# Longer pauses in the matmul order of a hybrid attention and linear-attention step: four places

## The chip, the cores and the metric

The kernel runs on one core of one Trainium2 chip. A core has a matrix engine (PE in the profile, with its weight loads as PEld), a vector engine (DVE), a scalar engine (ACT), a general engine (POOL), and a sync engine (SP) that issues most of the transfers. The metric is the time of one execution on the device, in microseconds (us). The times of several executions of the same program are compared by their median.

## The reference

One step of a layer with two groups of heads side by side. All arrays are float32; there are 2048 prompt rows and 32 rows of a running stream ("sample").

```python
n = rmsnorm(x)
z = n @ w_in                       # 1024 -> qa, ka, va, qg, kg, vg, rg, ca
# group A: 8 query heads, 2 key heads of 64; each chunk of 64 rows sees two chunks back
s = q @ k.T / 8 ; m = max(max(s), sink)
p = exp(s - m) ; a = p / (sum(p) + exp(sink - m)) @ v
# group B: 4 heads, keys of 64, values of 128; a decay for each key element
log_a = log_sigmoid(ca @ w_alpha + b_alpha) / 16
S = exp(log_a) * S + k v.T ; o = q S          # chunk-wise in the reference
g = rmsnorm(o) * silu(rg)
h = x + concat(a, g) @ w_out
y = h + relu(rmsnorm(h) @ w_up)**2 @ w_down   # 1024 -> 4096 -> 1024
```

The outputs are y for prompt and sample, the last keys and values, and the two states S.

## The kernel before

Rows are worked in tiles of 128: tile 0 to 15 are the prompt, tile 16 is the sample. A float32 product is made of three matmuls on pieces of the operands (high x high, high x low, low x high; names end in h and l). The program has four stages: attention (to about 372 us of the profiled execution), linear attention (to about 695 us), the output projection (to about 870 us), and the two layers of the feed-forward part.

**The order on PE is written at build time.** `self.clock` (L140 to L175) is a running sum of what the emitted matmuls should take, in ns. Large products (`gemm`, `gemm_wide`) call `tick()` after every few matmuls. Attention of a tile (`attend`, L607), a tile of linear attention (`gla_tile`, L990 and on) and the decay of a half (`decay`, L841) are generators: each `yield ns` is a pause, and `tick()` resumes a generator when `self.clock` has passed its due time. So a longer pause puts more matmuls of the large product that is running between two pieces of a generator. The order so made is fixed on PE by dependences between neighbours (`_pe`). The order on DVE, ACT, POOL and SP is made afterwards by a scheduler of the language, from the program as a whole; an engine runs its own list strictly in order. No instruction moves at run time.

**Attention.** For each tile the products zq, zkv and zr are made (query, key and value, gate), DVE normalizes queries and keys into qk and kn (L510, L512). `attend` then pauses (L608), transposes them (`qTp`, `kTp`), pauses, makes scores S for two chunks of 64 rows, each with the exponentials P on ACT behind the maxima and negm on DVE (L654, L655), and pauses after each chunk (L674). After a further pause come the transposes of P (pT), their copies to SBUF on ACT (pS), and the outputs O. S, pT, O and the small products of linear attention all live in one PSUM pool (`ps_s`) of five banks; a new tile in it waits until the readers of an older one are done. The large products use another pool (`ps_m`) of three.

**Linear attention.** It goes by halves of two tiles; half 0 has the sample tile as well. For a half, `project` makes zq, zk and zv. `decay` pauses (L855) and makes the gate logits la (two matmuls), which ACT and DVE turn into cc, a running sum (L871, L875). Each `gla_tile` then makes POOL, ACT and DVE build the arrays E from cc, q and k (L1023, L1034). On PE: small products dk for the diagonal, which DVE writes into AT (L1046); two transposes, also into the bank dk; 52 small matmuls A, which DVE masks into AT (L1099); a pause (L1104); and then go, the output, with v, AT, the query and the state. From go follow the new state (L1131), squares on ACT, a sum on DVE (L1138), an inverse root in many small steps (L256 to L261), and g (L1143), whose four operations are the last readers of go's two banks. After a long pause g is transposed (gTp). Several tiles are thus in flight, with DVE between most of their steps.

Of the kernel before, what the change touches and what calls it, by code (L numbers as in the profile page):

```python
# [66 lines left out]
class Builder:  # L67
# [240 lines left out]
    def attention_phase(self):  # L308
        tc, a, V, S, G, Q = self.tc, self.a, self.V, self.S, self.G, self.Q
        nt = self.nt  # L310
        w_in = a["w_in"].rearrange("(k p) n -> p k n", p=P)
        with ExitStack() as ctx:
# [103 lines left out]
            h, l = self.tok_pair("nT_0", 2 * P)  # L416
# [124 lines left out]
            def transposed_qk(t, qk, kn, ca):  # L541
                r = self.rows(t)
                pt = self.ps_s(f"qTp_{t}").rearrange("p (j t) -> p j t", j=4)[:, :, :r]
                for j in range(4):
                    self.tr(pt[:, j], qk[:r, j].rearrange("p v d -> p (v d)"))
                pk = self.ps_s(f"kTp_{t}")
                self.tr(pk[:, :r], kn[:r])
                self.tr(pk[:96, P : P + r], ca[:r].bitcast(F32))
                caT = wk.tile([96, P], F32, tag="caT", name=f"caT_{t}", bufs=1)
                V.tensor_copy(caT[:, :r], pk[:96, P : P + r])  # L550
                Q.dma_start(self.cad[t], caT[:, :r])
                return pt, pk[:, :r]
# [52 lines left out]
                self.store_mix(nt, slice(0, 4), aT)  # L605

            def attend(t, qk, kn, v, ca):  # L607
                yield 8500  # L608
                pt, pk = transposed_qk(t, qk, kn, ca)
                qT = wk.tile([P, 2, 4, 64], F32, tag="qT", name=f"qT_{t}")  # L610
                V.tensor_scalar(
# [18 lines left out]
                for ch in range(2):  # L630
# [36 lines left out]
                    for _, a0, m in parts[ch]:  # L667
# [3 lines left out]
                        if m == 64:  # L671
                            src, rb = (x.rearrange("p (v jp) k -> p v jp k", v=2) for x in (src, rb))
                        (G if ch == 0 else V).tensor_tensor(out=dst, in0=src, in1=rb, op=ALU.mult)  # L673
                    yield 3000  # L674
                yield 2000
                o = self.ps_s(f"O_{t}").rearrange("p (j t) -> p j t", j=4)
                for ch in range(2):
# [36 lines left out]
            for i, t in enumerate(order):  # L714
# [20 lines left out]
                if t == nt - 1:  # L735
# [5 lines left out]
                    Q.dma_start(self.rsd, rsT)  # L741
                    self.prepare_gla(0)
                self.spawn(attend_sample(*z.pop(t)) if t == nt else attend(t, *z.pop(t)))
                if t != nt - 2:
                    project_gate(t)
# [95 lines left out]
    def decay(self, h, tail=None):  # L841
# [10 lines left out]
        for t in tiles:  # L852
            Q.dma_start(ca[:, off : off + self.rows(t)].bitcast(F32), self.cad[t])
            off += self.rows(t)
        yield 5000 + 4000 * (h == 0)  # L855
        cc = self.cc[h] = self.mid.tile([P, 2, 288], F32, tag="cc", name=f"cc_{h}")
        if N <= 2 * P:
            x = self.ps_s(f"la_{h}")
# [20 lines left out]
    def gla_phase(self):  # L879
        tc, a, V, S, G, Q = self.tc, self.a, self.V, self.S, self.G, self.Q  # L880
        nt = self.nt
        with ExitStack() as ctx:
# [95 lines left out]
            def after(n, s):  # L978
                for _ in range(60):
                    if n < 0 or stage[n] >= s:  # L980
                        return
                    yield 500
                reach(n, s)
# [6 lines left out]
            def gla_tile(n, t, off, kq, cc):  # L990
# [9 lines left out]
                first = key == "p" and t == 0  # L1000
# [100 lines left out]
                                src[r].rearrange("s p (n m) -> s p n m", m=m),  # L1101
                            )
                stage[n] = 2
                yield 10000 if t != nt - 1 else 5000  # L1104
                yield from after(n - 1, 3)
                yield from after(n - 2, 4)

# [946 lines left out]
```

## Time and profile before

| what | value |
|---|---|
| median of 3 runs | 2169.01 us (2164.01 to 2177.4) |
| the profiled execution | 2172.5 us |
| its span, first to last instruction | 2170.7 us |
| mean granted PE clock | 0.992 |
| linear attention, 372 to 695 us: PE busy | 308.14 of 323.00 us |
| feed-forward, 870 to 2170.7 us: PE busy | 1286.57 of 1300.70 us |

The span is the time from the first to the last instruction of one execution that the profiler recorded; the execution took 1.8 us more than its span. A row of the page gives for a group of instructions the busy time, the mean of one, and the idle time of its engine just ahead of them with what ended it. In a timeline row the idle time stands in square brackets. The granted clock is a share of PE's full speed: at 0.50 every matmul takes twice its time.

### The profile page before, as it was taken

Reading aid. Unit: us, or ns where it says so; the run is one execution under the profiler, and the core shown is the slowest. Engines: PE = TensorE matmul, PEld = TensorE weight load, DVE = VectorE, ACT = ScalarE, POOL = GpSimd, SP = SyncE. Lnnn points to the kernel's source line nnn. Section 1 sums busy time; section 2 is a strip of 40 time slices with the busy share of each in tenths; the row PEclk is TensorE's granted clock in tenths of the full one; section 3 lists DMA queues with packets and bytes.
Section 4 is the critical chain, followed back from the end, with each engine's and each line's share of the span. In section 5 each row is a group of like instructions: output and inputs, shape, how many; then the busy total and the mean of one; then the engine's idle time right before and its main releaser. Section 6 shows DMA issues by size and latency. Waiting matters only on the chain.

```text
span 2170.7 us, 40621 instructions
## 1 busy us (share of the span) xinstructions
PE 2128.6 (98%) x14826; PEld 2002.9 (92%) x14826; DVE 1520.8 (70%) x3388; ACT 1231.6 (57%) x2737; POOL 1496.9 (69%) x1409
## 2 busy tenths in 40 slices
PE   8999999999998999999999999999999999999999
PEld 6777786788887999999999999999999999999999
DVE  7766766889997444677777775666666756776665
ACT  6554555565664222666665666656566666666663
POOL 1354445545553677889888786777887768888887
PEclk9999999999999999999999999999999999999999
DMA  8344565244435986765454467444444584445443
GB/s 287 128 159 133 188 209 170 104 166 143 158 104 162 378 325 273 284 194 164 154 158 161 136 211 249 130 140 130 140 146 127 179 286 136 139 149 155 145 127 108
DMA packets 189097, 381.81 MB, mean 176 GB/s; under 512 B 32209, under 2 KB 117378, under 8 KB 182114
## 3 DMA queue, kind: packets, MB, share of 16 engines
q1 hardware_dynamic: 154130, 323.10, 44.8%
q10 hardware_dynamic: 28208, 27.77, 3.7%
q0 software_dynamic: 6560, 28.35, 3.6%
q8 instruction: 117, 1.92, 0.4%
q14 instruction: 82, 0.67, 0.1%
HBM read 282.40 MB, written 96.76 MB: 175 GB/s over the span
## 4 chain that ended last, share of the span: by engine, by line
PE 87%; DVE 5%; DMA 4%; ACT 2%; issue 1%; POOL 1%; SPq 0%; ACTq 0%; DVEq 0%; POOLq 0%
PE dn L170 28%; PE u L170 27%; PE op L170 8%; PE zq L170 5%; PE zv L170 4%; PE zr L170 4%; PE zkv L170 2%; PE zk L170 2%; PE O L170 1%; PE go L170 1%; PE S L170 1%; PE A L170 1%; DVE AT L1099 1%; DMA stage<-in_w_in 1%; PE pT L174 1%
## 5 line engine op out<-in xcount | busy, mean ns | idle before, releaser
L1658 DVE TENSOR_TENSOR P<-P,dn 128x712 f32<-128x712 f32 (+1 forms) x612 | 534.5, 875 | 234.4 <-PE dn L170 218.1
L44 ACT ACTIVATE u<-u 128x356 f32<-128x356 f32 (+1 forms) x384 | 173.8, 453 | 43.5 <-PE u L170 23.2
L44 ACT ACTIVATE r<-u 128x356 f32<-128x356 f32 (+1 forms) x189 | 87.3, 462 | 132.0 <-PE u L170 131.9
L1658 DVE TENSOR_TENSOR u<-u,r 128x356 f32<-128x356 f32 (+1 forms) x144 | 75.7, 525 | 114.0 <-PE u L170 97.7
L1551 POOL TENSOR_TENSOR stage<-stage 128x512 f32<-128x512 f32 x90 | 117.0, 1300 | 22.5 <-DMA stage<-in_w_up 17.6
L1023 POOL TENSOR_TENSOR E<-cc 128x256 f32<-128x256 f32 (+1 forms) x117 | 70.0, 632 | 76.3 <-DVE cc L875 42.7
L792 POOL TENSOR_TENSOR sd<-sd 128x128 f32<-128x128 f32 (+2 forms) x132 | 94.5, 724 | 30.7 <-DMA sd<-in_w_down 26.6
L1099 DVE COPY_PREDICATED AT<-masks,A 64x64 f32<-64x64 int32 (+1 forms) x330 | 82.9, 253 | 16.1 <-ACT AT L44 5.8
L1658 DVE TENSOR_TENSOR uT<-u,uT 128x356 fp32r<-128x356 f32 (+1 forms) x183 | 89.9, 511 | 5.9 <-ACT uT L44 5.9
L44 ACT ACTIVATE uT<-u 128x356 fp32r<-128x356 f32 (+1 forms) x187 | 81.1, 457 | 3.0 <-DVE u L1658 2.8
L1658 DVE TENSOR_TENSOR uB<-u,uB 128x356 fp32r<-128x356 f32 (+1 forms) x141 | 72.3, 513 | 9.2 <-ACT u L44 8.5
L44 ACT ACTIVATE P<-S,negm 128x192 f32<-128x192 f32 (+2 forms) x128 | 51.6, 417 | 46.4 <-DVE negm L655 36.8
L44 ACT ACTIVATE op<-y 128x356 f32<-128x356 f32 (+1 forms) x42 | 19.4, 468 | 95.1 <-DVE y L1406 94.9
L1406 DVE TENSOR_TENSOR y<-op,y 128x356 f32<-128x356 f32 (+1 forms) x48 | 24.8, 529 | 67.0 <-PE op L170 62.7
L44 ACT ACTIVATE E<-E 128x1024 f32<-128x1024 f32 (+2 forms) x68 | 67.3, 1013 | 1.1
L44 ACT ACTIVATE uB<-u 128x356 fp32r<-128x356 f32 (+1 forms) x141 | 64.6, 458 | 2.9
L673 POOL TENSOR_TENSOR P<-P,es 128x512 f32<-128x512 f32 x15 | 15.5, 1036 | 68.3 <-ACT sq L44 27.2
L1034 DVE TENSOR_TENSOR E<-E,kq 128x256 f32<-128x256 f32 (+1 forms) x117 | 59.5, 561 | 0.7 <-ACT E L44 0.6
L44 ACT ACTIVATE pS<-pT 128x256 f32<-128x256 f32 (+1 forms) x62 | 27.2, 490 | 43.3 <-PE pT L174 43.3
L44 ACT ACTIVATE v<-go 128x256 f32<-128x256 f32 (+1 forms) x34 | 12.7, 380 | 65.5 <-DVE Sp L1131 34.6
L654 DVE TENSOR_REDUCE mx<-S 128x2 f32<-128x384 f32 (+2 forms) x64 | 32.8, 536 | 21.7 <-PE S L170 21.3
L619 POOL COPY VB<-v 64x64 f32<-64x64 f32 x64 | 16.2, 253 | 44.9 <-ACT v L44 42.8
(1574 smaller groups left out, 8181.7 us busy)
## 6 DMA issues: line engine op xcount, KB each, us to landing
stage<-in_w_up SPq DMA_DIRECT2D x90, 512.0 KB, 4.1
stage<-sd SPq DMA_DIRECT2D x86, 512.0 KB, 4.5
stage<-in_w_down SPq DMA_DIRECT2D x43, 512.0 KB, 3.3
stage<-su SPq DMA_DIRECT2D x30, 512.0 KB, 4.2
stage<-in_w_down SPq DMA_DIRECT2D x47, 256.0 KB, 3.3
sd<-sd POOLq DMA_DIRECT2D x11, 1024.0 KB, 4.6
x1a<-in_x_prompt SPq DMA_DIRECT2D x16, 512.0 KB, 5.7
su<-stage SPq DMA_DIRECT2D x15, 512.0 KB, 3.6
```

What stands on the lines that cost most here:

```text
L44: ins = f(*args, **kw)
L170: self._pe(self.T.matmul(out, lhsT, rhs, start=start, stop=stop, **kw), ns)
L174: self._pe(self.T.transpose(out=out, in_=in_, identity=self.ident[:r, :r]), 109)
L619: G.tensor_copy(vb[hp, ch, cs], v[ch * 64 : ch * 64 + 64, cs])
L654: V.reduce_max(mx[:, ch, us], sp, axis=AX.X)
L792: self.after(self.G.tensor_tensor(out=o, in0=x, in1=y, op=op), self.last_pe)
L1023: G.tensor_tensor(out=e4, in0=c4, in1=ref, op=ALU.subtract)
L1034: V.tensor_tensor(out=e4, in0=e4, in1=halves_of(kq, L, m), op=ALU.mult)
L1099: V.copy_predicated(dst, mk.unsqueeze(1).broadcast_to([L // nh, 2, w // m, m]), src[r].rearrange("s p (n m) -> s p n m", m=m),)
L1406: V.tensor_tensor(out=y[:, f], in0=ps, in1=y[:, f], op=ALU.add)
L1551: tt = lambda o, x, y, op: G.tensor_tensor(out=o, in0=x, in1=y, op=op)
L1658: add = lambda out, x, y, op=ALU.add: V.tensor_tensor(out=out, in0=x, in1=y, op=op)
```

## The change

Four pauses get longer. That of the first tile ahead of its transposes goes from 8500 to 12500 ns; that after the two score chunks of the last tile from 3000 to 5500; that ahead of the gate logits from 5000 to 6500 for all halves but the first, which keeps 9000; and that ahead of go of prompt tile 0 from 10000 to 13000.

```diff
             def attend(t, qk, kn, v, ca):
-                yield 8500
+                yield 8500 if t else 12500
                 pt, pk = transposed_qk(t, qk, kn, ca)
...
-                    yield 3000
+                    yield 3000 if t < nt - 1 else 5500
...
-        yield 5000 + 4000 * (h == 0)
+        yield 6500 + 2500 * (h == 0)
...
-                yield 10000 if t != nt - 1 else 5000
+                yield 5000 if t == nt - 1 else 13000 if first else 10000
```

No instruction is added or taken away. The pauses move matmuls on PE from the start of attention to the start of the output projection, and the scheduler then orders DVE, ACT and POOL anew in that stretch. In the rows below, names carry the tile's number (S_15_1_0 is tile 15, chunk 1, key head 0; go0_1 is the first bank of go of tile 1; the last number only tells buffers apart), an arrow points from what is read to what is written, and the sizes are those of the result.

PE around the transposes of tile 0, before and then after:

```order
L170 MATMUL zr_1_600<-wr1h_246,nT_0l_281 128x512
L174 MATMUL qTp_0_622<-packed_201,qk_0_434 128x128 x4
L174 MATMUL kTp_0_627<-packed_201,kn_0_514 128x128
L174 MATMUL kTp_0_627<-packed_201,CA0_380 96x128
L170 MATMUL zr_1_600<-wr1h_246,nT_0h_280 128x512
```

```order
L170 MATMUL zq_2_658<-wq1h_240,nT_2l_573 128x512
L174 MATMUL qTp_0_674<-packed_201,qk_0_434 128x128 x4
L174 MATMUL kTp_0_679<-packed_201,kn_0_514 128x128
L174 MATMUL kTp_0_679<-packed_201,CA0_380 96x128
L170 MATMUL zq_2_658<-wq1h_240,nT_2h_572 128x512
```

The transposes moved behind the last three matmuls of zr of tile 1 and the first fifteen of zq of tile 2.

PE around the scores of the second chunk of tile 15, before and then after:

```order
L174 MATMUL pT_14_1_128_4446<-packed_201,P_14_1_4297 128x128 x4
L174 MATMUL pT_14_1_64_4453<-packed_201,Pb_14_1_4317 128x128 x2
L170 MATMUL S_15_1_0_4460<-kW_15_4337,qT_15_4331 128x192
L170 MATMUL S_15_1_1_4461<-kW_15_4337,qT_15_4331 128x192
L170 MATMUL S_15_1_0_4460<-kW_15_4337,qT_15_4331 128x192
L170 MATMUL S_15_1_1_4461<-kW_15_4337,qT_15_4331 128x192
L170 MATMUL zq_0_0_4425<-nTb_0h_4415,wqgh_4195 128x288
```

```order
L170 MATMUL zq_0_0_4425<-nTb_0h_4415,wqgl_4195 128x288
L170 MATMUL S_15_1_0_4472<-kW_15_4336,qT_15_4330 128x192
L170 MATMUL S_15_1_1_4473<-kW_15_4336,qT_15_4330 128x192
L170 MATMUL S_15_1_0_4472<-kW_15_4336,qT_15_4330 128x192
L170 MATMUL S_15_1_1_4473<-kW_15_4336,qT_15_4330 128x192
L170 MATMUL O_14_4359<-pS_14_1_128_4451,v_14_4033 64x4x64 x2
```

Twelve zq of linear attention's half 0 stand between pT of tile 14 and these scores, and O of tile 14 follows them at once. The transposes pT of tile 15, which stood ahead of la and 18 zk, now stand behind these, with O of tile 15 straight behind each pair of pT.

DVE around g of prompt tile 0 (the operations that release the banks of go of tile 0), before and then after:

```order
L261 SCALAR_TENSOR_TENSOR rsq_y_g0_5198<-go0_0_5182,rsq_y_g0_5198 128x4
L1034 TENSOR_TENSOR E_2_1_5293<-E_2_1_5293,kq_1_4900 128x256 x3
L1030 TENSOR_TENSOR E_2_1_5293<-E_2_1_5293,kq_1_4900 128x256
L1143 SCALAR_TENSOR_TENSOR g_0_4625<-go0_0_5182,rsq_y_g0_5198,g_0_4625 128x128
L1143 SCALAR_TENSOR_TENSOR g_0_4625<-go1_0_5183,rsq_y_g0_5198,g_0_4625 128x128
```

```order
L1046 COPY_PREDICATED AT1_4613<-packed_201,dk_2_5378 128x512
L261 SCALAR_TENSOR_TENSOR rsq_y_g0_5298<-go0_0_5282,rsq_y_g0_5298 128x4
L1034 TENSOR_TENSOR E_3_0_5338<-E_3_0_5338,kq_1_4900 128x256 x4
L259 TENSOR_TENSOR go0_0_5282<-go0_0_5282,rsq_y_g0_5298 128x4
L260 SCALAR_TENSOR_TENSOR go0_0_5282<-go0_0_5282,rsq_y_g0_5298 128x4
L1034 TENSOR_TENSOR E_3_1_5349<-E_3_1_5349,kq_1_4900 128x256 x3
L261 SCALAR_TENSOR_TENSOR rsq_y_g0_5298<-go0_0_5282,rsq_y_g0_5298 128x4
L1030 TENSOR_TENSOR E_3_1_5349<-E_3_1_5349,kq_1_4900 128x256
L1143 SCALAR_TENSOR_TENSOR g_0_4625<-go0_0_5282,rsq_y_g0_5298,g_0_4625 128x128
L1143 SCALAR_TENSOR_TENSOR g_0_4625<-go1_0_5283,rsq_y_g0_5298,g_0_4625 128x128
```

g of tile 0 stood ahead of the E of tile 3 and of the diagonal copy (L1046) of tile 2; now it stands behind both. On PE go of tile 0 moved from the middle of A of tile 1 to behind all 52 of them and nine zv.

PE around the last transposes into the bank dk of tile 3, before and then after:

```order
L170 MATMUL zq_2_1_5598<-nTb_2h_4893,wqgh_4195 128x256
L170 MATMUL zq_2_1_5598<-nTb_2l_4894,wqgh_4195 128x256
L170 MATMUL zq_2_1_5598<-nTb_2h_4893,wqgl_4196 128x256
L174 MATMUL dk_3_5521<-packed_201,E_3_1_5349 128x128 x2
L170 MATMUL A0_3_5628<-E_3_0_5338 64x64
```

```order
L170 MATMUL A1_2_5432<-E_2_1_5258 64x32
L170 MATMUL la_2_5556<-caf_2_5372,wal_2880 128x256 x2
L170 MATMUL dk_3_5568<-ones_2882,qkp_3_5332 64x2 x4
L174 MATMUL gTp_0_5576<-packed_201,g_0_4625 128x128 x4
L174 MATMUL dk_3_5568<-packed_201,E_3_1_5349 128x128 x2
L170 MATMUL A0_3_5591<-E_3_0_5338 64x64
```

Thirty zq of half 2 stood between A of tile 2 and these transposes; now A of tile 2, la, the diagonal, gTp of tile 0 and the transposes follow one another, and the thirty zq come behind A of tile 3. In the halves after that, la stands six zq later than before.

## The prediction

> **What bounds the kernel now.** I read the page first (who is busy, the chain that ended last), then PE's busy time and granted clock by stretches, then PE's timeline at its gaps, then the other engines around each gap.
>
> ```profile
> span 2170.7 us, 40621 instructions
> PE 2128.6 (98%) x14826; PEld 2002.9 (92%) x14826; DVE 1520.8 (70%) x3388; ACT 1231.6 (57%) x2737; POOL 1496.9 (69%) x1409
> PE 87%; DVE 5%; DMA 4%; ACT 2%; issue 1%; POOL 1%; SPq 0%; ACTq 0%; DVEq 0%; POOLq 0%
> ```
>
> TensorE is busy for 98% of the span. The change adds and removes no matmul, so it can only win PE's idle time (42 us in all) and the stretches in which PE runs at half clock. Each row of the next view is one stretch: its limits, its length, busy time of PE, PEld, DVE, ACT and POOL (instructions in brackets), PE's granted clock, DMA share, GB/s.
>
> ```profile
> 372.00:695.00 323.00, 308.14 (x3568) 262.87 (x3567) 278.50 (x898) 189.63 (x352) 164.28 (x220) 0.97 0.41 136
> ...
> 37.63:41.04 3.41, 1.34 (x7) 1.17 (x8) 3.37 (x8) 0.25 (x1) 1.86 (x2) 1.00 0.00 0
> 41.04:44.45 3.41, 3.41 (x10) 2.66 (x9) 3.13 (x13) 0.62 (x2) 0.29 (x1) 0.50 0.61 175
> 348.24:351.65 3.41, 1.15 (x9) 0.86 (x7) 2.30 (x7) 1.31 (x7) 0.31 (x1) 1.00 1.00 347
> 351.65:358.48 6.83, 6.73 (x25) 4.72 (x24) 5.42 (x11) 5.57 (x18) 3.93 (x3) 0.50 0.63 217
> 409.68:413.09 3.41, 1.56 (x44) 1.16 (x44) 3.03 (x17) 0.38 (x1) 2.42 (x3) 1.00 0.27 72
> 413.09:423.33 10.24, 9.61 (x90) 7.93 (x91) 7.34 (x27) 5.63 (x13) 5.95 (x10) 0.50 0.53 194
> 546.21:549.62 3.41, 1.89 (x20) 1.74 (x21) 3.38 (x10) 2.22 (x8) 2.54 (x4) 1.00 0.84 342
> 549.62:553.04 3.42, 3.42 (x19) 3.42 (x18) 3.04 (x14) 2.93 (x5) 0.00 (x0) 0.50 0.50 129
> ...
> 870.20:873.61 3.41, 2.03 (x12) 1.71 (x11) 1.91 (x3) 1.67 (x3) 3.41 (x4) 1.00 0.98 355
> 873.61:877.02 3.41, 1.93 (x12) 1.96 (x13) 2.19 (x13) 1.64 (x4) 3.41 (x4) 1.00 1.02 418
> ```
>
> Four times the same pair: a stretch of 3.41 us with 1.5 to 2.3 us of PE idle at full clock, and behind it one to three such lengths at clock 0.50. In 870.20 to 873.61, 1.38 us idle is followed by full clock. So here the limit lies near 1.5 us of idle in one stretch. At half clock the same matmuls need twice the time, so a half-clock stretch costs half of its PE time: 1.7, 3.4, 4.8 and 1.7 us, 11.6 in all. The first row says the other thing that counts: DVE is busy 278.5 of the 323 us of linear attention (86%), so DVE is near its own limit there.
>
> These are the gaps at the four places (start, duration, engine, what, in square brackets the idle time before it and what ended it):
>
> ```profile
> 36.02 0.66 PE L174 MATMUL qTp<-packed,qk 128*128 128x128 f32 x4 [0.45 <-DVE qk L510]
> 39.70 0.33 PE L174 MATMUL kTp<-packed,kn 128*128 128x128 f32 x1 [3.02 <-DVE kn L512]
> ...
> 351.31 2.45 PE L170 MATMUL S<-kW,qT 64*128 64x192 f32 x8 [2.26 <-ACT P L44]
> ...
> 413.72 1.65 PE L170 MATMUL go<-v,AT 128*128 128x128 f32 x6 [2.47 <-DVE g L1143]
> ...
> 547.73 0.47 PE L170 MATMUL la<-caf,wal 96*128 96x256 f32 x2 [1.89 <-ACT AT L44]
> ```
>
> They add up to 3.47 + 2.26 + 2.47 + 1.89 = 10.1 us, with the clock 21.7 us: the ceiling, 1.0% of the span.
>
> **The change, place by place.** Prices of filler that moves into a gap:
>
> ```profile
> 541.59 0.39 PE L170 MATMUL zv<-wvg1h,nTb_4h 128*128 128x512 f32 x1
> 541.82 0.39 PE L170 MATMUL zv<-wvg1l,nTb_4h 128*128 128x512 f32 x1
> ...
> 543.46 0.28 PE L170 MATMUL zq<-nTb_5l,wqgh 128*128 128x256 f32 x1
> 543.58 0.28 PE L170 MATMUL zq<-nTb_5h,wqgl 128*128 128x256 f32 x1
> ...
> 445.87 1.82 PE L170 MATMUL A<-E 64*64 64x64 f32 x104
> ```
>
> A 512-wide matmul starts 0.23 us after the last, a 256-wide one 0.12 us; all A of one tile take 1.82 us.
>
> (a) *Transposes of tile 0.* Three zr and fifteen zq of tile 2 (18 x 0.23 = 4.1 us) move ahead of them, more than the 3.47 us of wait, so both waits go, and the 1.7 us of half clock with them: 5.2. But zq of tile 2 needs both halves of its input, and POOL makes the low half late:
>
> ```profile
> 35.95 3.54 POOL L349 TENSOR_TENSOR nT_2l<-xT1a,nT_2h 128x512 fp32r<-128x512 f32 x2 [3.93 <-ACT nT_2h L44]
> ```
>
> Its first half is there at 35.95 + 1.77 = 37.7; PE wants it at about 36.7: a new wait of 1.0 (between 0 and 1.8, where the second half also decides). Behind that, tile 0's scores now stand among tile 1's (four groups of S with 9 zr, 2 us, between them; they were spread over 10 us) and the scores of tile 2 stand straight behind transposes whose PSUM copies they need. The nearest rows are the 2.26 us that S waits for P above and the 0.87 us of a pair of copies below; I take 2.7 for these (0 to 5). Net +1.5 (-1.6 to +5.2).
>
> (b) *Second chunk of tile 15.* Twelve zq (some 0.13 us each, 1.6) move between the transposes and S.
>
> ```profile
> 351.54 0.42 ACT L44 ACTIVATE P<-S,negm 128x192 f32<-128x192 f32 x1
> ...
> 367.09 0.87 ACT L44 ACTIVATE pS<-pT 128x512 f32<-128x512 f32 x2 [1.03 <-PE pT L174]
> ```
>
> S still cannot start before 351.3 (it needs the banks that the exponentials of chunk 0 read), so 2.26 becomes 0.7, and its second half waits for the last exponential, 351.96: another 0.5. Gain 1.1. That idle is under 1.5 us, so the 3.4 us of half clock should go; I count 2.5. In return both O of tile 15 lose the zk that stood ahead of them and wait for the copies of the row above, 0.65 each: -1.3. Net +2.3 (-1.5 to +5.7).
>
> (c) *First output of linear attention.* go of tile 0 moves behind all of A of tile 1 and nine zv, la of the next half 20 A later. At 413.7 go finds g of the sample tile done: the 2.47 and the 4.8 of half clock go, 7.3. What is late next:
>
> ```profile
> L1099 DVE COPY_PREDICATED AT<-masks,A 64x64 f32<-64x64 int32 (+1 forms) x330 | 82.9, 253 | 16.1 <-ACT AT L44 5.8
> ```
> ```profile
> 412.82 1.10 DVE L1143 SCALAR_TENSOR_TENSOR g<-go,rsq_y_g,g 32x128 f32<-32x128 f32 x4
> 413.85 0.74 DVE L1002 TENSOR_TENSOR qkp<-kq 128x256 f32<-128x256 f32 x2
> 416.47 0.61 DVE L1131 SCALAR_TENSOR_TENSOR Sp<-Sp,ec,go 128x128 f32<-128x128 f32 x2 [1.88 <-PE go L170]
> ...
> 430.68 1.12 DVE L1143 SCALAR_TENSOR_TENSOR g<-go,rsq_y_g,g 128x128 f32<-128x128 f32 x4
> ...
> 434.02 1.15 DVE L1034 TENSOR_TENSOR E<-E,kq 128x256 f32<-128x256 f32 x3
> ```
> ```profile
> 435.19 0.49 PE L170 MATMUL go<-Sp,Qc 64*128 64x128 f32 x4
> ...
> 445.56 0.38 PE L174 MATMUL dk<-packed,E 128*128 128x128 f32 x2
> ```
> ```profile
> 435.60 0.84 ACT L44 ACTIVATE cc<-la,packed 128x256 f32<-128x256 f32 x2 [0.46 <-PE la L170]
> ...
> 438.43 0.68 ACT L44 ACTIVATE v<-go 128x256 f32<-128x256 f32 x2
> ...
> 441.99 1.23 ACT L44 ACTIVATE AT<-A 64x128 f32<-64x128 f32 x6 [1.57 <-PE A L170]
> ```
>
> On DVE the four g of tile 0 now stand behind all E of tile 3. From 414.6: 20 masks 5.1, two Qc 0.8, eight E of tile 2 3.1, Sp 0.6, the sum 0.7, eleven small steps 2.0, one diagonal copy 0.7, eight E of tile 3 3.1, g 1.1: it ends at 431.7, as before (431.8); the 1.88 of idle DVE saved has gone into tile 3's work. PE is there by 413.8 + 1.4 (go) + 39 x 0.23 + 18 x 0.12 + 1.5 (dk, A) = 427.8, so the transposes of g of the sample tile and go of tile 1, whose banks g frees, wait about 3.9 us. Next la and the diagonal of tile 3 share a bank: the second waits for cc, behind two squares (0.7), six AT (1.2) and cc (0.8): 2.5. The transposes of g of tile 0 then need a bank that the masks of A of tile 2 free: on DVE sum 0.7, small steps 1.7, 18 masks 4.6, diagonal copy 0.7 after the squares, some 5 us more. So dk of tile 3 comes at about 443, against 445.56, but 30 zq (3.6 us) that came ahead of it are still to run: 1 us behind the old time in work done, though the old time held the whole gap and half clock. Idle of 3.9 and 7.5 us halves the clock again: 1.2 on go of tile 1 and 3.4 after 443, with 0.4 for AT. Net -6 (-12 to +7.3, the upper end if DVE keeps none of these waits).
>
> (d) *la of the later halves* moves behind six zq, 0.7 us, and g of tile 7 stands one E multiply earlier (0.4): 1.89 becomes 0.8. With 1.1 us less the stretch keeps its clock: +1.1 +1.7 = +2.8 (0 to 3.6). Other halves had no wait there.
>
> Sum: 1.5 + 2.3 - 6 + 2.8 = +0.6 us of gain. The profiled execution took 2172.5 us (1.8 around its span), 3.5 above the median of 2169.01. So 2171.9 against 2172.5, or 2168 against the median: no change that can be measured. About 1%, 21.7 us, is what a measurement of this kernel can tell.
>
> [...]
>
> **Rivals.**
> 1. *All four places are cleared, nothing waits in their place*: 2169 - 21.7 = 2147. For it: the filler exceeds each wait at (a), nearly at (b). Against it: DVE at 86%, and (c) puts more DVE work ahead of g.
> 2. *(c) comes out even or better*, because the waits are shorter than summed and PE's filler runs while DVE works: with (c) at 0 to +5 the time is 2157 to 2162.
> 3. *Slower*: (c)'s chain g, la, A masks costs its low end, 12 us (two idle stretches of over 3 us, five half-clock lengths). It decides as soon as (c) loses more than the 6.6 us of the others: 2174.
> 4. *The half clock does not follow these gaps* and its stretches stay where they are or come back elsewhere, so the gains of clock at (a), (b), (d), 5.9 us, fall away: 2174. [...]
>
> **How the numbers follow.** Forecast (2163 to 2172) 0.42; rival 1 0.06; rival 2 0.27; rival 3 0.15; rival 4 0.10. Leaving out rival 1, and a tenth at the slow end, the range is 2156 to 2178. Faster by over 1% is most of rival 1, 0.05; slower by over 1% needs more than any of these, 0.03; within 1% 0.92.
>
> **What would show it.** Right: no idle before kTp of tile 0 and none of 2 us before S of tile 15; full clock around 351 to 358 and 549 to 553; about 4 us of idle before gTp or go of tile 1 released by DVE L1143, and more before gTp of tile 0 released by L1099, with half clock behind. Wrong: go of tile 1 without a wait (then rival 2 or 1), half clock still at the four old places (rival 4), or gaps of over 3 us in tiles 4 to 15, which I expect unchanged.

## The result: slower by 0.6%

The changed kernel took 2185.13 us (median of 13 runs, 2177.42 to 2191.84) against 2171.16 us (13 runs, 2164.01 to 2178.22) for the kernel before. The ratio is 1.0058 with a 95% interval of 1.0044 to 1.0073: slower by 12.6 us. (The ratio is not the quotient of the two medians; these lie 14.0 us or 0.64% apart, inside the interval.) That is within the 1% that a measurement of this kernel was said to tell, but with intervals this narrow it is a real loss, and the median lies 7 us above the range of the forecast.

### The profile after

The head of the page of the changed kernel:

```profile
span 2175.5 us, 40638 instructions
PE 2128.2 (98%) x14826; PEld 2003.2 (92%) x14826; DVE 1524.1 (70%) x3388; ACT 1230.9 (57%) x2737; POOL 1499.2 (69%) x1409
PE 80%; DVE 9%; DMA 5%; ACT 3%; issue 2%; POOL 1%; SPq 0%; ACTq 0%; DVEq 0%; POOLq 0%
```

The profiled execution is the fastest of the 13 (2177.42 us), and its span is only 4.8 us longer than that of before. A loss of the measured size is there all the same, ahead of the feed-forward part. The first matmul of that part, before and then after, starts 11.7 us later:

```profile
867.45 0.33 PE L170 MATMUL u<-B11h,wf_u0A 128*128 128x356 f32 x1
```
```profile
879.12 0.33 PE L170 MATMUL u<-B11h,wf_u0A 128*128 128x356 f32 x1
```

From there to the end of the span it takes 1303.3 us before and 1296.4 after. No changed pause lies in this part, and over the 19 profiles of this document it takes between 1296 and 1311 us, so a difference of some us between two spans says nothing by itself.

PE's busy time is the same to 0.4 us. What moved is the chain that ended last: DVE's share of it went from 5% to 9%.

To see where, I take what PE waited for between 372 and 750 us, linear attention and the first part of the output projection. Each row has the waiting operation, what it waited for, the total in us, how often, and the longest. Before:

```profile
PE dk L174 <- DVE AT L1046: 6.2, 3, 4.2
PE go L170 <- DVE g L1143: 2.5, 1, 2.5
PE la L170 <- ACT AT L44: 1.9, 1, 1.9
```

and after:

```profile
PE dk L174 <- DVE AT L1046: 8.3, 5, 3.4
PE gTp L174 <- DVE AT L1099: 4.7, 1, 4.7
PE dk L174 <- DVE rsq_y_g L261: 2.3, 1, 2.3
PE oprb L170 <- DVE rsq_y_y L261: 1.9, 1, 1.9
PE gTp L174 <- DVE g L1143: 1.8, 1, 1.8
PE A L170 <- DVE g L1143: 1.5, 1, 1.5
PE dk L170 <- ACT cc L44: 1.5, 1, 1.5
```

The two waits that the pauses aimed at, go for g and la for AT, are gone. Six others of 1.5 us and more stand in their place, five of them on DVE. One of them, oprb for the inverse root rsq_y_y, is not in linear attention at all.

The same on PE's timeline of the changed kernel (start, duration, operation; the idle time before it in brackets):

```profile
37.28 0.50 PE L170 MATMUL zq<-wq0h,nT_2l 128*128 128x512 f32 x1 [0.94 <-POOL nT_2l L349]
...
193.31 0.65 PE L170 MATMUL O<-pS,v 128*64 128x256 f32 x4 [1.66 <-ACT pS L44]
...
351.47 0.59 PE L170 MATMUL S<-kW,qT 64*128 64x192 f32 x2 [0.67 <-ACT P L44]
...
362.76 0.65 PE L170 MATMUL O<-pS,v 128*64 128x256 f32 x4 [1.04 <-ACT pS L44]
...
426.99 0.66 PE L174 MATMUL dk<-packed,E 128*128 128x128 f32 x2 [2.31 <-DVE rsq_y_g L261]
...
430.90 0.60 PE L174 MATMUL gTp<-packed,g 32*128 32x32 f32 x4 [1.83 <-DVE g L1143]
...
440.37 0.60 PE L170 MATMUL dk<-ones,qkp 128*64 128x2 f32 x8 [1.46 <-ACT cc L44]
445.71 1.09 PE L174 MATMUL gTp<-packed,g 128*128 128x128 f32 x4 [4.75 <-DVE AT L1099]
...
563.20 0.68 PE L174 MATMUL dk<-packed,E 128*128 128x128 f32 x2 [2.67 <-DVE AT L1046]
...
726.70 1.68 PE L170 MATMUL oprb<-packed,rsq_y_y 82*128 82x82 f32 x8 [1.88 <-DVE rsq_y_y L261]
```

And the stretches around the places where the clock fell, of the changed kernel; one more, 6.83 us from 665.64, has its like before (6.83 us from 655.44) and is left out (limits, length, busy time of PE, PEld, DVE, ACT and POOL, PE's granted clock, DMA share, GB/s):

```profile
351.48:358.31 6.83, 6.62 (x45) 5.66 (x46) 4.60 (x8) 5.05 (x15) 3.97 (x3) 1.00 0.57 222
191.19:194.60 3.41, 1.61 (x10) 0.73 (x8) 2.93 (x14) 2.98 (x7) 1.54 (x2) 1.00 0.16 30
194.60:198.02 3.42, 3.42 (x16) 2.80 (x16) 3.18 (x12) 1.31 (x4) 2.78 (x5) 0.50 0.40 102
423.30:426.71 3.41, 1.39 (x12) 1.18 (x10) 3.17 (x11) 2.85 (x4) 1.27 (x2) 1.00 0.97 344
426.71:450.60 23.89, 15.57 (x254) 13.02 (x254) 15.86 (x60) 8.66 (x20) 2.03 (x4) 0.50 0.25 79
559.83:563.24 3.41, 0.74 (x7) 0.54 (x6) 3.16 (x10) 0.00 (x0) 0.00 (x0) 1.00 0.04 12
563.24:566.66 3.42, 3.42 (x104) 3.09 (x106) 2.39 (x5) 0.38 (x1) 1.14 (x2) 0.50 0.02 5
727.08:730.50 3.42, 3.42 (x16) 3.42 (x16) 2.08 (x5) 0.45 (x1) 3.42 (x3) 0.50 1.00 406
```

The 6.83 us of half clock behind S of tile 15 are gone, as forecast. The 3.41 us that stood at 549.62 are gone too, but 3.41 us come back at 563.24, behind the new wait of 2.67 us. Between 426.71 and 450.60 PE runs at half clock for 23.9 us in one piece, seven lengths of 3.41, with 15.57 us of work in them: 7.8 us lost to the clock alone.

Since PE's work is the same in both kernels, the loss can be kept as a ledger: idle time, and half of the work done at half clock. PE in the kernel before, at clock 0.50 and then at 1.00:

```profile
422.22 0.63 PE L170 MATMUL zv<-wvg0h,nTb_1h 128*128 128x512 f32 x1
422.64 0.63 PE L170 MATMUL zv<-wvg0l,nTb_1h 128*128 128x512 f32 x1
...
424.35 0.39 PE L170 MATMUL zv<-wvg1l,nTb_1h 128*128 128x512 f32 x1
424.58 0.39 PE L170 MATMUL zv<-wvg1h,nTb_1l 128*128 128x512 f32 x1
```

A 512-wide matmul starts about 0.43 us after the last at 0.50 and 0.23 at 1.00, 1.9 times; a 256-wide one 0.21 (before, from 549.81) and 0.12, 1.8 times; all A of one tile take 3.50 us (after, from 447.17) and 1.82, 1.9 times. So not every matmul takes twice its time, as the section on the profile before and the prediction have it, and half is slightly too much. I keep it, as the forecast counted with it. The same two stretches, before

```profile
405.00:425.00 20.00, 17.07 (x176) 14.49 (x175) 16.23 (x62) 7.91 (x17) 13.55 (x22) 0.74 0.34 119
425.00:450.00 25.00, 24.39 (x360) 21.31 (x359) 21.28 (x73) 16.73 (x34) 12.24 (x18) 1.00 0.36 124
```

and after

```profile
405.00:425.00 20.00, 19.32 (x210) 16.17 (x208) 18.95 (x61) 15.03 (x25) 14.91 (x20) 1.00 0.43 142
425.00:450.00 25.00, 14.97 (x242) 12.48 (x245) 17.36 (x67) 9.23 (x21) 1.43 (x3) 0.53 0.31 105
```

Before, 3.5 us of these 45 us were idle and 4.8 were lost to half clock (the 9.61 us of work that the prediction shows): 8.3. After, 10.7 were idle and 7.8 lost to the clock: 18.5. So this stretch, in which the go pause (place (c) of the prediction) acts, became 10.2 us worse. Counted in the same way, the stretch from 30 to 372 us won 4.0 us, that from 450 to 700 lost 1.4 and that from 700 to 870 lost 4.2; with the 10.2 this makes 11.8, close to the 11.7 above. So these 45 us hold most of the loss; that it is the go pause which brings it is shown below, by the kernel without it.

### The profile page after: what moved, and what is told of

It is laid out like the page before. It is cut to its first block, busy times and chain, and to the rows that moved or that the text cites. A ratio compares the mean times of both kernels' runs of the same rounds, so it can differ in the third digit from the quotient of the medians.

```text
span 2175.5 us, 40638 instructions
## 1 busy us (share of the span) xinstructions
PE 2128.2 (98%) x14826; PEld 2003.2 (92%) x14826; DVE 1524.1 (70%) x3388; ACT 1230.9 (57%) x2737; POOL 1499.2 (69%) x1409
## 4 chain that ended last, share of the span: by engine, by line
PE 80%; DVE 9%; DMA 5%; ACT 3%; issue 2%; POOL 1%; SPq 0%; ACTq 0%; DVEq 0%; POOLq 0%
PE dn L170 28%; PE u L170 28%; PE op L170 7%; PE zr L170 3%; PE zq L170 3%; DVE AT L1099 3%; PE zv L170 2%; PE zkv L170 2%; DVE E L1034 1%; PE O L170 1%; PE S L170 1%; PE go L170 1%; DMA stage<-in_w_in 1%; PE zk L170 1%; PE A L170 1%
## 5 line engine op out<-in xcount | busy, mean ns | idle before, releaser
L1099 DVE COPY_PREDICATED AT<-masks,A 64x64 f32<-64x64 int32 (+1 forms) x330 | 82.7, 253 | 19.2 <-ACT AT L44 9.2
```

Of the source, the lines that this page charges most:

```text
L1099: V.copy_predicated(dst, mk.unsqueeze(1).broadcast_to([L // nh, 2, w // m, m]), src[r].rearrange("s p (n m) -> s p n m", m=m),)
```

## The experiments

All 17 runs of experiments are told here; each ratio is that to the kernel before on the same chip, with its 95% interval. Place (a) is the pause of the first tile, (b) that of the last tile's chunks, (c) that ahead of go of tile 0, (d) that ahead of la.

| places changed | ratio | interval | wait of oprb, us |
|---|---|---|---|
| (a), (b), (c), (d): the changed kernel | 1.0058 | 1.0044 to 1.0073 | 1.88 |
| (a) | 0.9999 | 0.9985 to 1.0013 | none |
| (b) | 1.0002 | 0.9987 to 1.0018 | 0.91 |
| (c) | 1.0044 | 1.0025 to 1.0062 | none |
| (d) | 1.0074 | 1.0058 to 1.0091 | 2.36 |
| (d), halves 1 and 2 only | 1.0021 | 1.0004 to 1.0038 | none |
| (d), halves 3 to 7 only | 1.0032 | 1.0011 to 1.0053 | 2.26 |
| (a), (b) | 0.9978 | 0.9963 to 0.9992 | none |
| (a), (b), (d) | 1.0010 | 0.9988 to 1.0031 | none |
| (c), (d) | 1.0067 | 1.0042 to 1.0093 | 3.40 |

### One place at a time

Each of these kernels is the kernel before with one line of the change.

```diff
-                yield 8500
+                yield 8500 if t else 12500
```

> Only the first tile's pause (12500). Theory 1 (what is won at the first tile is given back in the attention stage, where ACT's copies pT of tile 7 stand behind a step that waits for a transfer of x): the 3.5 us gap and the half clock near 41 us go, a wait of 1 us for POOL comes, a gap of 1.5 to 2 us with a half-clock length comes near 192 us; time 0 to 1 us under before, ratio 0.998 to 1.001. Rival (the gain is kept): 4 us less, ratio 0.998 or lower, no gap near 192 us.

Measured: 2169.62 us against 2172.07, no difference that can be told. The idle time before kTp and the half clock behind it are gone from its profile, but a wait of 1.90 us for pS ends at 193.41, as in the changed kernel (1.66 us, to 193.31) and in every other profile with (a), and in none without it. ACT's timeline of the changed kernel shows why:

```profile
191.62 1.06 ACT L44 ACTIVATE x1a<-x1a 128x1024 f32<-128x1024 f32 x1 [1.00 <-DMA x1a<-in_x_prompt]
...
192.68 0.58 ACT L44 ACTIVATE pS<-pT 128x512 f32<-128x512 f32 x1
```

The copy pS stands behind an activation of x1a that waits for its transfer; in the kernel before it stands ahead of it. In the changed kernel half clock from 194.60 comes with it; in this run's own profile the wait has none behind it. Part of what (a) won is so given back 150 us later.

```diff
-                    yield 3000
+                    yield 3000 if t < nt - 1 else 5500
```

> Only the last tile's pause (5500). Theory 1: gap ahead of S of tile 15 from 2.3 to 0.7 us, half clock at 351 to 358 us gone, two new waits of 0.5 to 1 us ahead of O of tile 15; 3 us less, ratio 0.9975 to 0.9995. Rival (the half clock stays, or the gain is lost behind): ratio 1.000.

Measured: 2173.12 us against 2172.07, none either, as the rival had it. S waits 0.65 us instead of 2.26 and no half clock follows; O of tile 15 waits 1.61 us in its place.

```diff
-                yield 10000 if t != nt - 1 else 5000
+                yield 5000 if t == nt - 1 else 13000 if first else 10000
```

> Only the pause ahead of go of prompt tile 0 (13000). Theory 1 (this pause puts g of tile 0 behind the E of tile 3 on DVE): waits of 3 to 4 us in sum ahead of dk of tile 2, gTp of the sample tile and go of tile 1 near 427 to 432 us, half clock behind; but thirty zq stay ahead of dk of tile 3, so the wait of 5 us there is missing; 2 to 6 us more, ratio 1.001 to 1.003. Rival (the la pause makes the loss): 2 to 5 us less, since the gap near 411 us and its half clock are gone, ratio 0.998 to 0.999.

Measured: 2179.97 us against 2172.07. dk of tile 2 waits 0.96 us, gTp of the sample tile 2.68 for g, the diagonal 0.90, and 13.65 us of half clock follow. These waits are those expected, but the loss, 0.44%, is above the expected 0.1 to 0.3%. By the ledger, the stretch from 405 to 450 us loses 11.5 us here (5.1 idle and half of the 12.76 busy at half clock) against 8.3 before, so most of what (c) costs alone lies elsewhere. Its profile has 10.24 us of half clock from 624.76, where before has full clock; the rest was not traced. There is no wait of gTp for masks here: la stands ahead of go of tile 1, not between A of tile 2 and gTp, and gTp of tile 0 takes its bank without a wait. Only the kernels with (c) and (d) together have the wait of 4.75 us.

```diff
-        yield 5000 + 4000 * (h == 0)
+        yield 6500 + 2500 * (h == 0)
```

> Only the pause ahead of the gate logits (6500). Theory 1 (both pauses of linear attention share the loss): la, the diagonal of tile 3, gTp of tile 0 and dk of tile 3 stand next to one another as in the changed kernel, so the wait for the masks of A of tile 2 is there, 3 to 5 us with half clock, but go of tile 1 does not wait for g; 3 to 7 us more, ratio 1.001 to 1.003. Rival (this pause alone makes the loss): 9 to 13 us more, ratio 1.004 to 1.006.

Measured: 2186.51 us against 2172.07 (6 runs): alone, the pause ahead of la costs at least as much as the whole change. Neither expectation holds: the wait for the masks of A of tile 2 is not there, and the loss is larger than the 0.4 to 0.6% of the rival. Three of its new waits on PE:

```profile
558.58 0.44 PE L174 MATMUL dk<-packed,E 128*128 128x128 f32 x2 [2.14 <-DVE AT L1046]
...
596.67 0.44 PE L174 MATMUL dk<-packed,E 128*128 128x128 f32 x2 [1.60 <-DVE AT L1046]
```
```profile
727.54 2.00 PE L170 MATMUL oprb<-packed,rsq_y_y 82*128 82x82 f32 x8 [2.36 <-DVE rsq_y_y L261]
```

My reading is that a later la makes cc, and all that DVE builds from it, later against PE's list, so that PE catches DVE at the diagonal copy; the rows fit it, but no run tests it. More than these waits costs what follows them:

```profile
597.86:604.69 6.83, 6.83 (x92) 6.32 (x86) 5.07 (x19) 4.95 (x11) 5.70 (x10) 0.50 0.15 41
```

This profile (of the slowest of the 6 runs) has half clock at 440.85 (6.83 us), here and at 679.78 (3.41 us), where before has full clock; the other profile with (d) alone, that with the moved addition below, has it at 440.84, 594.44 and 676.36 for the same lengths. With 16.44 and 16.49 us of work in them, that is 8.2 us lost to the clock in either. The wait at oprb, with 6.83 us of half clock behind it, is taken up below. To see in which halves the cost lies, the pause was lengthened in some only:

```diff
-        yield 5000 + 4000 * (h == 0)
+        yield 5000 + 4000 * (h == 0) + 1500 * (h in (1, 2))
```

> The pause ahead of the gate logits is 6500 for halves 1 and 2 alone. Theory 1 (the loss of that pause comes where tiles 1 to 3 stand, near 410 to 447 us: la, the diagonal of tile 3, gTp of tile 0 and dk of tile 3 in a row): 7 to 12 us more, ratio 1.003 to 1.006. Rival (it comes in the later halves and at the start of the output projection): at most 4 us more, ratio under 1.002.

```diff
-        yield 5000 + 4000 * (h == 0)
+        yield 5000 + 4000 * (h == 0) + 1500 * (h > 2)
```

> The pause ahead of the gate logits is 6500 for halves 3 to 7 alone. Theory 1: 2 to 6 us more, ratio 1.001 to 1.003, from waits of dk for L1046 and of oprb near 725 us. Rival: 9 to 14 us more, ratio 1.004 to 1.0065.

Measured: 2176.19 and 2178.0 us against 2171.55. Both parts cost something, 0.21% and 0.32%, so neither group of halves carries the loss alone. The first ratio lies just over the rival's 1.002 and under the theory's 1.003 to 1.006; the second lies just over its theory's 1.001 to 1.003.

### Combinations

The kernel before with the first two lines of the change, (a) and (b):

```diff
-                yield 8500
+                yield 8500 if t else 12500
...
-                    yield 3000
+                    yield 3000 if t < nt - 1 else 5500
```

> The two pauses of attention (tile 0 and last tile) together, without the two of linear attention. If the gains that the single traces show up to the feed-forward part are real: 3 to 6 us less, ratio 0.997 to 0.9987. Rival (they are given back later): ratio 0.9995 to 1.001.

Measured: 2167.73 us against 2171.55, faster by 0.22%, as expected if the gains are real. Neither could be told alone, but the single intervals reach down to 0.9985 and 0.9987, so the runs don't contradict one another.

The changed kernel with (c) put back:

```diff
-                yield 5000 if t == nt - 1 else 13000 if first else 10000
+                yield 10000 if t != nt - 1 else 5000
```

> The changed kernel with the pause ahead of go of tile 0 put back to 10000 (transposes of tile 0, last tile and gate logits as changed). Theory: the gate logits' pause carries the loss, the two attention pauses give about 0.2% and the go pause adds little once the logits are late; then the ratio to the kernel before is 1.005 to 1.0075 (the logits alone 1.0074 less 0.0022), so putting the go pause back does not help. Rival: the go pause carries the loss, 10 us of it; then the ratio is 1.000 to 1.002.

Measured: 2172.93 us against 2170.41. The rival was right and my theory of that moment fell: of the whole change (c) carries 0.48% (1.0058 less 1.0010, 10.4 us). In the same stretch of this kernel (windows as above):

```profile
405.00:425.00 20.00, 19.14 (x211) 16.36 (x211) 18.76 (x66) 16.09 (x26) 14.30 (x19) 1.00 0.38 127
425.00:450.00 25.00, 21.47 (x333) 18.64 (x332) 22.65 (x83) 11.45 (x28) 11.75 (x19) 0.86 0.33 118
```

4.4 us are idle and at most 3.5 (0.14 of 25) lost to the clock: 7.9, as before the change, and 10.6 less than with (c). Against (a) and (b) alone, la still costs it 0.32%.

The changed kernel with (a) and (b) put back:

```diff
-                yield 8500 if t else 12500
+                yield 8500
...
-                    yield 3000 if t < nt - 1 else 5500
+                    yield 3000
```

> The changed kernel with both attention pauses put back (only the go pause and the gate logits' pause as changed). Theory: the two attention pauses win 0.2% with or without the others; then the ratio is 1.007 to 1.009, 0.2% above the changed kernel. Rival: the attention pauses win nothing here; then it is 1.005 to 1.0065, as the changed kernel.

Measured: 2186.28 us against 2170.41 (6 runs), between the two expectations: the interval of the changed kernel and this one's overlap, so whether (a) and (b) win anything beside (c) and (d) can't be told.

### Why the transposes of g wait

The theory of the prediction is that g of tile 0 comes late because eight multiplications E of tile 3 stand ahead of it on DVE. In the changed kernel they were given to POOL:

```diff
-                            V.tensor_tensor(out=ev, in0=ev, in1=k, op=ALU.mult)
+                            (G if t == 3 else V).tensor_tensor(out=ev, in0=ev, in1=k, op=ALU.mult)
...
-                        V.tensor_tensor(out=e4, in0=e4, in1=halves_of(kq, L, m), op=ALU.mult)
+                        (G if t == 3 else V).tensor_tensor(out=e4, in0=e4, in1=halves_of(kq, L, m), op=ALU.mult)
```

> The changed kernel with the eight E multiplies of tile 3 on POOL instead of DVE (the same products, order on PE unchanged). Theory 1 (g of tile 0 comes late because it stands behind them on DVE): the wait ahead of gTp of the sample tile, 1.8 us in the changed kernel, falls under 0.5, that ahead of gTp of tile 0 (4.75 us, behind the masks of A of tile 2) stays within 1.5 us of its size unless dk of tile 3 waits for POOL; ratio 1.002 to 1.005 to before. Rival (PSUM and PE order, not the DVE list, make the waits): the waits at 427 to 446 us stay in sum, ratio 1.005 to 1.008.

Measured: 2182.51 us against 2172.4, 1.0046 (1.0032 to 1.0061; 5 runs). PE's waits in this kernel:

```profile
427.81 0.54 PE L174 MATMUL gTp<-packed,g 32*128 32x32 f32 x4 [0.32 <-DVE g L1143]
...
442.56 1.09 PE L174 MATMUL gTp<-packed,g 128*128 128x128 f32 x4 [4.75 <-DVE AT L1099]
```

The wait for g fell from 1.83 to 0.32, that of dk of tile 2 from 2.31 to 1.19: the theory holds for these. The wait of 4.75 us is untouched, and so has another cause. DVE's timeline of the changed kernel shows it:

```profile
429.89 1.12 DVE L1143 SCALAR_TENSOR_TENSOR g<-go,rsq_y_g,g 128x128 f32<-128x128 f32 x4
436.37 0.61 DVE L1131 SCALAR_TENSOR_TENSOR Sp<-Sp,ec,go 128x128 f32<-128x128 f32 x2 [5.35 <-PE go L170]
...
444.31 1.25 DVE L1099 COPY_PREDICATED AT<-masks,A 64x64 f32<-64x64 int32 x4
```

PE and DVE wait for each other in turn. PE waits until g is done (431.01); then DVE has nothing for 5.35 us, while PE, at half clock, does go of tile 1; then DVE needs 9 us for the sum, the small steps and 18 masks; and for these PE waits 4.75 us. Each wait prepares the next, and the clock stays at 0.50 until 450.60.

One more kernel gave POOL one multiplication of each tile of the kernel before, to see whether less DVE work helps as such:

```diff
-                            V.tensor_tensor(out=ev, in0=ev, in1=k, op=ALU.mult)
+                            G.tensor_tensor(out=ev, in0=ev, in1=k, op=ALU.mult)
```

> The kernel before with the last of the eight E multiplies of every tile on POOL. If DVE's load is what bounds linear attention: the waits of dk and go for DVE (about 9 us with the one at 652 us) get shorter, 2 to 6 us less, ratio 0.997 to 0.999. Rival (POOL's list now waits for ACT and makes the next E late, or the load of DVE bounds nothing): 0 to 8 us more, ratio 1.000 to 1.004.

Measured: 2174.58 us against 2172.4, 1.0011 (0.9996 to 1.0026). No gain can be told. The lists of DVE and POOL changed in many other places with it, so this says little about a lighter DVE with the rest as it was.

### The wait at the output projection

No step of the prediction had a cost there. DVE's timeline of the changed kernel:

```profile
722.53 0.17 DVE L260 SCALAR_TENSOR_TENSOR oprb<-oprb,rsq_y_y 82x4 f32<-82x4 f32 x1
725.49 0.50 DVE L1409 TENSOR_TENSOR acc<-acc,op 128x328 f32<-128x328 f32 x1 [2.79 <-ACT op L44]
...
726.49 0.16 DVE L261 SCALAR_TENSOR_TENSOR rsq_y_y<-oprb,rsq_y_y 82x4 f32<-82x4 f32 x1
```

Seven small steps of the root are done by 722.7. Then an addition (L1409) that has nothing to do with the root waits 2.79 us for ACT, and the last four steps, 0.8 us of work, stand behind it. In the lists of all kernels with this wait the addition stands with only three or four of the root's steps behind it; in all without it and with the addition unmoved, the kernel before among them, it stands directly after L257, early enough to be over. DVE worked its list in order here: the next step of the root had its input at 722.70 and stood until 725.90 behind an addition that waited 2.79 us. The scheduler set the list at build time; why it put the addition there was not looked into.

So this one addition was moved: the sum of the second column block now comes after that of the third.

```diff
                 if f:
-                    V.tensor_tensor(out=acc, in0=acc, in1=ps, op=ALU.add)
+                    if j != 1 or f != 1:
+                        V.tensor_tensor(out=acc, in0=acc, in1=ps, op=ALU.add)
+                    if j == 1 and f == 2:
+                        V.tensor_tensor(out=acc, in0=acc, in1=held, op=ALU.add)
+                    held = ps
```

In the changed kernel:

> The changed kernel with one addition on DVE moved: the sum acc of the second column block of the output projection (op_1_1, L1409) comes after that of the third, so that it no longer stands inside the inverse root rsq_y_y on which the transposes oprb wait. Theory: the wait of 1.88 us ahead of oprb is an accident of DVE's list (acc waits 2.79 us for ACT there, and the last four steps of the root stand behind it); then it goes with the half clock behind it, 1.7 us, and the ratio to the kernel before falls from 1.0058 to 1.004 to 1.0045. Rival: DVE is late there because linear attention ended late, whatever its list; then the wait stays and the ratio is 1.0055 to 1.006.

In the kernel with (d) alone:

> The kernel with the gate logits' pause alone (1.0074) with the same addition moved. Theory: its wait of 2.36 us ahead of oprb and 6.83 us of half clock behind it go, 5.8 us; then the ratio is 1.0045 to 1.0055, the rest being its waits at the diagonal transposes of linear attention. Rival: 1.007 or more.

Measured: 2178.88 us against 2169.68 and a ratio of 1.0044 (1.0029 to 1.0059; 6 runs) in place of 1.0058; and 2175.97 us, 1.0036 (1.0020 to 1.0053) in place of 1.0074. PE goes from op to oprb without a pause in both; in the first:

```profile
728.17 0.31 PE L170 MATMUL op<-m1h,wo01l 128*128 128x328 f32 x1
728.32 1.02 PE L170 MATMUL oprb<-packed,rsq_y_y 82*128 82x82 f32 x8
```

The wait is that of the list, as the theory said: PE's and ACT's lists are the same in both, and it is gone. The gain in the first kernel is of the expected size, though the intervals overlap; in the second it is larger than expected, and the two intervals (1.0058 to 1.0091, and 1.0020 to 1.0053) don't overlap: about half of what (d) cost alone is this accident.

### Other values of the pause ahead of la

If a later la is bad, an earlier one may be good.

```diff
-        yield 5000 + 4000 * (h == 0)
+        yield 3500 + 5500 * (h == 0)
```

> The pause ahead of the gate logits goes the other way, from 5000 to 3500. If a later la is what makes DVE late, an earlier one gives time back or costs nothing but a longer wait ahead of la: 4 us less to 2 us more, ratio 0.998 to 1.001. Rival (any new order costs, since the old one fits the waits of DVE): 5 to 12 us more, ratio 1.002 to 1.0055.

Measured: 2167.2 us against 2171.55, 0.9981 (0.9963 to 1.0000). With (a) and (b) as well:

> The two pauses of attention as in the change, the pause ahead of the gate logits 3500 instead of 6500, go of tile 0 as before. If the single gains add: 7 to 11 us less than before, ratio 0.995 to 0.997. Rival (they share the same luck of half clock): 3 to 6 us less, ratio 0.9972 to 0.9986.

Measured: 2170.47 us against 2172.4, 0.9999 (0.9983 to 1.0014); the gains did not add up, and oprb waited 1.46 us. With (a) and (b), and la earlier still, at 2000:

```diff
-        yield 5000 + 4000 * (h == 0)
+        yield 2000 + 7000 * (h == 0)
```

> As the run before with the pause ahead of the gate logits at 2000. If an earlier la goes on relieving DVE: as the run before or 2 to 4 us less, ratio 0.993 to 0.996. Rival (the wait ahead of la, which needs the banks that g of the tile before frees, grows by the matmuls taken away): 3 to 8 us more than the run before, ratio 0.998 to 1.001.

Measured: 2202.49 us against 2172.4, 1.0129 (1.0106 to 1.0153; 6 runs), far beyond both expectations. Now A waits for the masks, in four halves in a row, 2.2 to 3.3 us each, and oprb 4.14; the first of them:

```profile
519.33 2.95 PE L170 MATMUL A<-E 64*64 64x64 f32 x97 [2.22 <-DVE AT L1099]
```

With (a) and (b) the ratios are 1.0129 at 2000, 0.9999 at 3500, 0.9978 at 5000 and 1.0010 at 6500; without them 0.9981 at 3500 and 1.0074 at 6500. So 2000 and 6500 lose, and between 3500 and 5000 no run tells a difference. Last, (a), (b) and 3500 with the addition moved as above:

> Both attention pauses as changed and the gate logits' pause at 3500 (0.9999, with a wait of 1.46 us ahead of oprb), with the same addition moved. Theory: the wait goes; its profile had no half clock behind it, so 1.5 to 3 us, 0.9985 to 0.9992. Rival: no difference, 0.9995 to 1.0005.

Measured: 2164.85 us against 2169.68, 0.9977 (0.9962 to 0.9992): faster than the kernel before, but with (a) and (b) alone at 0.9978 it can't be called better than that. The gain over 3500 without the moved addition (0.9999) is larger than the theory's, but the intervals overlap.

## Why the prediction was wrong

**(a) and (b), forecast +1.5 and +2.3 us: right in sum, in part by luck.** Together they won 0.22%, 4.8 us (1.7 to 8.0). The new waits came where forecast: 0.94 us for nT_2l (1.0), 0.67 us ahead of S (0.7), 1.04 and 0.47 us ahead of the two O (0.65 each). The 2.7 us that I took at (a) for the scores behind the transposes did not come: between 30 and 190 us the list of PE's waits in the changed kernel has nothing but the one for nT_2l. Not forecast was the wait for pS at 193.31, 1.66 us, with 3.42 us of half clock behind it, 1.7 us lost. That these two errors nearly cancel is luck.

**(c), forecast -6 us: the mechanism right, the size wrong.** This is one of the two steps that failed. Every link was there: g behind E of tile 3, the diagonal behind cc, gTp behind the masks, and half clock. The wait of 3.9 us came as two, 2.31 and 1.83; the 7.5 us as 1.46 and 4.75. The waits were 10.35 us in all, against 11.4. The half clock took 7.8 us, against the 5.0 that I counted: I let it follow two idle stretches separately, and it held through the whole chain. The larger slip was in the sum. The terms as I had them, 7.3 won, 11.4 of new waits, 5.0 of half clock, give -9.1. I wrote -6, which is 1 us and the 5.0 of half clock, because I went by the time at which one instruction (dk of tile 3, forecast for 443, measured 446.59) would come, and took off the work that PE had still to do; a ledger of idle time and half clock, as in the section on the result, would have said -9, and -10.2 was measured. With -9.1 the forecast would have been 2171.5 and rival 3's condition met: (c) losing more than the others' 6.6 us is what happened. By runs (c) costs 10.4 us, but that holds the wait at oprb as well, and an interval of about 5 to 16 us, estimated from those of the two ratios, does not separate them.

**(d), forecast +2.8 us: the wrong sign.** This is the other step that failed, and the larger miss. Beside (a) and (b) it cost 0.32% (1.0010 against 0.9978), 7 us, with an interval that reaches close to zero; alone, without the accident at oprb, 0.36% (0.20 to 0.53). The 1.89 us and the half clock at 549 went, as forecast, but in the changed kernel the same length of half clock came back at 563.24. The sentence "Other halves had no wait there" was the failure: no wait in the trace of before is not slack. In the changed kernel PE waits for AT of L1046 five times, 8.3 us in all, against three times and 6.2 (the 2.67 us ahead of dk at 563.20 are new, and before had one of 4.2). In both profiles with (d) alone new half clock stands at three places of linear attention and loses 8.2 us, against the 1.7 that went. That the later cc, E and AT of each half bring it is my reading of the rows; which of them decides was not tested.

**The wait at oprb: no step had it.** It is a rearrangement of DVE's list far from the edited lines. From the changed kernel with and without the moved addition it costs 0.14%, about 3 us, though the two intervals overlap; it came in with (c) here (it is not in the kernel with (a), (b) and (d)) and with (d) elsewhere.

By runs the sum is 4.8 - 7 - 10.4 = -12.6 us, of which 3 are that of oprb, against the +0.6 of the forecast. Of the 13.2 us between them, 9.8 are (d) and 4.4 (c), less the 1.0 that (a) and (b) won beyond their forecast. These shares belong to this order of adding. In another order they differ: (d) alone is 0.74%, (c) added to it changes nothing that can be told (1.0067). That the accident at oprb then counts once, and that waits of (c) and (d) fall together, would explain it, but was not shown. How much of the rest comes from such rearrangements of DVE's list was not settled.

**Rival 4 was partly right.** Half clock followed gaps, but not each of them and not by one limit. In the profile of before its stretches up to 700 us start at 41.04, 351.65, 413.09, 549.62 and 655.44. These lie 310.61, 61.44, 136.53 and 105.82 us apart: 91, 18, 40 and 31 times the length of one step, which comes to 3.413 us. In that of the changed kernel they start at 194.60, 426.71, 563.24, 665.64 and 727.08, by the same step 68, 40, 30 and 18 times apart. In the kernel with (d) in halves 3 to 7 the unchanged wait of 2.26 us ahead of S of tile 15 was followed by full clock. These rows (windows) follow that execution's own steps of 3.41 us, counted on from a half-clock stretch earlier in it:

```profile
347.04:350.46 3.42, 1.72 (x12) 1.01 (x8) 3.21 (x7) 0.40 (x2) 0.92 (x2) 1.00 0.98 374
350.46:353.87 3.41, 2.63 (x16) 1.94 (x18) 1.72 (x6) 3.12 (x13) 1.15 (x2) 1.00 1.02 374
```

The gap lies across the limit at 350.46, 1.70 us of idle in one stretch, 0.56 in the next. In the profile of before the whole wait lay in one stretch (348.24 to 351.65), and the same 2.26 us brought 6.83 us of half clock there and none here. That its place against the steps decides is my reading; no run tests it. But a wait of about 2 us had no fixed price. The limit of 1.5 us of idle that the prediction took does not hold either. In the profile with (a), (b) and (d), 1.11 us of idle (513.40 to 516.82) was followed by half clock, and 1.89 us (649.94 to 653.35) by full clock.

**The signs named.** "No idle before kTp", "none of 2 us before S" and "full clock around 351 to 358 and 549 to 553" came true. Of the waits at g I had named the release by L1143 and by L1099, and both are there. "Gaps of over 3 us in tiles 4 to 15" did not come new, but smaller ones did, and they were the sign that counted.

## What to carry to other kernels

Where PE's work stays the same, keep a ledger of idle time and half clock for the whole stretch, and trust its sum over the arrival time of one instruction. A stage in which the vector engine is 86% busy need not have slack because no wait is seen: here a pause 1.5 us longer in seven halves brought waits and half clock where there had been none. And where a scheduler orders the other engines, an edit can turn up hundreds of microseconds away as a ready step behind a waiting one (here at 726.70 us, 1.88 us of PE's time, some 280 us behind the stretch of (c)); look there, in the engine's own list, before explaining a loss by the edited lines. And where two profiles differ by a few us, compare them up to the end of the part that was changed: here the untouched feed-forward part hid 6.9 us.

## What was not expected of the hardware

PE stayed at half clock for 23.89 us without a break while it was busy for 15.57 of them, 65%; in the trace of before no such stretch was longer than 10.24 us. One of its seven lengths was busy from end to end, and half clock went on behind it:

```profile
433.54:436.95 3.41, 3.41 (x44) 2.63 (x45) 0.58 (x2) 0.38 (x1) 0.00 (x0) 0.50 0.23 60
```

The limit at which the clock falls is not sharp in these views: a stretch of 3.41 us with 1.52 us of idle brought it (546.21, shown in the prediction), one with 1.80 did (191.19), one with 1.70 did not (347.04, above); over the other profiles it lies anywhere between 1.1 and 1.9 us (513.40 and 649.94, above).
